# Second feed-forward product: operands split at the producer and stored as pairs, Winograd sums gathered in PSUM, the output gate applied to the sums

## The chip, the core and the metric

One core of one Trainium2 chip. TensorE (PE) multiplies into PSUM, VectorE (DVE) and ScalarE (ACT) read PSUM and SBUF, GpSimd (POOL) reads SBUF only, and DMAs are issued from the queues of SyncE (SP), ScalarE and GpSimd. The metric is the device time of one execution in microseconds (us), the median of several runs.

## The reference, cut to what matters

The kernel is one layer of a token mixer (three mixers, gated sum, projection) and then this part, which the change is about:

```
def swiglu(xn, w_in, w_out):
    gate, up = jnp.split(xn @ w_in, 2, axis=-1)
    return (jax.nn.silu(gate) * up) @ w_out
...
h_lat = h_lat + gt2l * swiglu(modulate(rms_norm(h_lat, norm2), sh2l, sc2l), w_ffn_in, w_ffn_out)
return rms_norm(h_lat, norm_f)
```

There are 1024 tokens, 1024 channels and 2816 hidden columns, all float32.

## The kernel before

Each float32 operand of a matmul is split into two parts, high (a rounded copy, ACT) and low (value minus high, DVE), by `split2` (L1475). A product is then three matmuls for each 128 rows: high by high, high by low, low by high.

Both feed-forward products use Strassen's scheme in Winograd's form: a 2 by 2 block product from seven block products and additions.

**First product**, `ffn_in` (L1553). The 2816 hidden columns go by in 11 pairs of column tiles. `quad(m, w)` makes the gate half (w = 0) or the other half (w = 1) of a pair: seven products of 12 matmuls, each in a PSUM bank of its own, 168 matmuls a pair. DVE adds the products (L1626 to L1649), ACT applies silu, POOL multiplies the halves (L1608). `hidden` (L1588) forms the seven left operands of the second product from the four hidden blocks and stores them to DRAM (`hid_d`) as float32, on SP's queue.

**Second product**, `ffn_out` (L1666). The 11 pairs are the inner dimension, taken in GROUPS of 2, 3, 3 and 3 pairs. In a group there are four steps t, each a tile of 128 tokens from each half of the tokens. A step has seven products p1 to p7 of 3 matmuls a pair: 42 matmuls in a step of the first group, 63 in the others, 924 in all. `weights(i)` (L1680) loads a pair's rows, multiplies them by the gate row `bc1` on POOL (L1685), forms sums on POOL and splits seven operands. `hidden(i, t)` (L1709) loads a pair's seven left operands for a step in three pieces (`hraw`), and splits each piece into `hh` again, in every step. DVE adds up the products (L1778 to L1791), and POOL or DVE adds the result into `acc` (L1752), which starts as the residual from DRAM. The last group adds squares, the norm and the store of the output.

In step 0 of a group the products run pair by pair into seven banks, so that the first pair can start before the others' weights are there. In the other steps they run product by product.

The instruction order of each engine is set by a scheduler which works on estimated durations; each engine then runs its list strictly in order.

Of the kernel before, what the change touches and what calls it, by code (L numbers as in the profile page):

```python
# [16 lines left out]
P = 128  # L17
# [8 lines left out]
def vb(ap, n):  # L26
    """[128, a] -> [128, a, n] with a step-0 last dim."""
    return ap.unsqueeze(len(ap.shape)).to_broadcast(list(ap.shape) + [n])


def mb(ap, n):
    """[128, a...] -> [128, n, a...] with a step-0 middle dim."""
    sh = list(ap.shape)
    return ap.unsqueeze(1).to_broadcast([sh[0], n] + sh[1:])


class SplitMixin:
    def split(s, raw, hi, lo):
        """exact split of an fp32 tile into two fp32r parts, the columns (g, c) in the order (c, g)"""
        h, l = (t.rearrange("p k (c g) -> p k g c", c=16) for t in (hi, lo))  # L40
        raw = raw.rearrange("p k (g c) -> p k g c", c=16)
        s.nc.scalar.activation(h, raw, AF.Copy)
        s.nc.vector.tensor_tensor(l, raw, h, op=ALU.subtract)
        return hi, lo
# [143 lines left out]
def _parts(v, bits):  # L188
    """v as a sum of fp32 constants, all but the last with few significant bits"""
# [12 lines left out]
class S5Mixin:  # L202
    def s5_setup(s, pool, fpool, tpool):
# [45 lines left out]
        def exp_parts(x, em, ex):  # L249
            """ex = exp(x), em = exp(x) - 1"""  # L250
# [81 lines left out]
        def cmul(pr, pi, o, n_, a, b):  # L332
            """pr, pi: [o, o + n_) = [a, a + n_) times b"""
# [50 lines left out]
    def s5_u(s, q, pool, w):  # L384
        """in-projection tile of u to DRAM as [tau][(c, g)][(half, w) of the latents, chunk of the context], in pieces"""
# [103 lines left out]
    def s5_scan(s, pool):  # L489
        """scan within five blocks of 32 chunks at once, then over the blocks' ends"""  # L490
# [17 lines left out]
    def s5_carry(s, e, pool):  # L508
        """the states of blocks 1 to 4 of groups 4 e .. 4 e + 3 from those before the blocks"""
# [15 lines left out]
    def s5_toeplitz(s, h, pool):  # L525
        """within-chunk responses of half h of the groups"""
# [5 lines left out]
    def s5_back(s, e, pool):  # L532
        """outputs of groups 4 e .. 4 e + 3"""
# [35 lines left out]
    def s5_out(s, pool):  # L569
        """skip, gelu and the gated unit in the token order (t, h, w); yields between the split of the input and the products"""  # L570
# [65 lines left out]
class RwkvMixin:  # L636
    def rwkv_const(s, pool):
        """small constants that live until the last chunk step"""
# [49 lines left out]
    def shift(s, m, ctx, pool, tag, bufs=1):  # L688
        """in-projection tile m of zb after the token shift"""
# [205 lines left out]
    def rwkv_inverse(s, aq, pool, tag, E):  # L895
        """rows of -A^T on (direction, head parity, j) x unit x t -> rows of ((I + A)^-1)^T"""
# [23 lines left out]
    def rwkv_chain(s, pool, halfway):  # L920
        """the chunks in order, both directions side by side, a chunk of each in a piece"""
# [43 lines left out]
        def flush(i):  # L965
            """second halves of the outputs whose first halves were two steps ago"""
# [94 lines left out]
    def rwkv_out(s, b, ysum, pool):  # L1061
        """group norm of tokens 128 b .. 128 b + 127, then the output gate, feature-major"""
# [31 lines left out]
WTB = 6  # L1094
TV = 1
WSEQ = "w n0 w n1 n2 n3 f s0 f s1 f s2 f f s3"
AVE = (((0, 0),), ((0, 1), (1, 0)))
HB, OTB = {2: 7, 3: 4}, 5
# [15 lines left out]
class Kern(LruMixin, S5Mixin, RwkvMixin, ParamMixin, SplitMixin):  # L1114
# [9 lines left out]
    def fill(s, n, after=None):  # L1124
        """the next n pieces of the background work, behind an instruction of the tensor engine if one is given"""
# [30 lines left out]
    def front(s, pool, wpool, side, parts):  # L1156
        """normed, modulated and transposed input as split parts, with pieces of other work at its side"""
# [95 lines left out]
    def mod2(s, pool):  # L1253
        """gates of both residuals (as rows in DRAM) and the second modulation, in pieces"""
# [33 lines left out]
    def wsplit(s, src, nk, pool, tag, rb=1, hb=1, lb=1, pool_hi=False, pool_lo=False):  # L1288
        """split parts of a weight tile"""
# [11 lines left out]
    def mm3(s, ps, whi, wlo, ahi, alo, nk):  # L1301
        """ps = sum over k of w[k]^T a[k] from the split parts"""
# [4 lines left out]
    def mm3s(s, ps, whi, wlo, ahi, alo, nk):  # L1307
        """the same in pieces of three, yields between them"""
# [9 lines left out]
    def in_wp(s, m, pool):  # L1318
        """split parts with the columns (g, c) in the order (c, g)"""
# [15 lines left out]
    def zg(s):  # L1335
        """the gates of the branches, in pieces of three matrix products"""
# [15 lines left out]
    def half(s, ap, h):  # L1352
        """tokens 256 .. 767 (h = 0) or the others of [128, 1024]"""
# [4 lines left out]
    def branch_y(s, y_d, h):  # L1358
        """split parts of half h of a branch input: [:, 0] and [:, 1]"""
# [10 lines left out]
    def branch(s, br, m, h, w, yt, wpool, out=None):  # L1370
        """gated product of a branch for half h of the tokens, in pieces of three matrix products"""
# [12 lines left out]
    def branches(s, acc, y0, wpool):  # L1384
        """the branches a and c, their gated sum to acc[m][half]"""
# [12 lines left out]
    def branch_b(s, h, acc, mg, wpool):  # L1398
        """last branch for half h of the tokens: split parts of the merged branches"""
# [12 lines left out]
    def yb_part(s, b, o):  # L1412
        """split parts of block b of the second half of the tokens"""
# [6 lines left out]
    def yb_last(s):  # L1420
        """the blocks 1 and 6, before 0 and 7 come straight from the chain"""
# [16 lines left out]
    def row_bc(s, pool, j):  # L1438
        """row of a gate (0, 1) or of the last norm (2) on every partition"""
# [7 lines left out]
    def wo_load(s, ring, quarters):  # L1447
        """split parts of the output weights, s.wo[half of the columns][row tile] = (hi, lo)"""
# [26 lines left out]
    def split2(s, raw, hl, eng=None):  # L1475
        """split parts (hi, lo) of a tile"""
# [4 lines left out]
    def wout(s, h, mg, wpool):  # L1481
        """output projection of half h of the tokens onto the residual; yields after two products"""
# [17 lines left out]
    def wnorm(s, h, t, wpool, parts, y):  # L1500
        """second norm of a token tile, modulated and transposed, to y(q)"""
# [29 lines left out]
    def wsum(s, t, wpool, parts, y):  # L1531
        """sums of the halves for a token tile"""
# [20 lines left out]
    def ffn_in(s, parts, ring, epool, tp):  # L1553
        """hidden tiles of the feed-forward, by Strassen's scheme (Winograd's form) on halves of the tokens, halves of
        the rows and pairs of column tiles; yields between the first products, then after a pair"""
# [4 lines left out]
        def product(b, name):  # L1560
            ps = s.mm()
            hi, lo = parts(name)
            seq = [(w, a, k) for k in range(4) for w, a in ((b[0], hi), (b[0], lo))] + [(b[1], hi, k) for k in range(4)]
            for n, (w, a, k) in enumerate(seq):
                nc.tensor.matmul(ps, w[:, k], a[:, k], start=n == 0, stop=n == len(seq) - 1)  # L1565
# [16 lines left out]
        def etmp():  # L1582
            return epool.tile([P, 512], F32, name="fe", tag="fe", bufs=4)

        def tmp(pool=None):
            return (pool or s.tl).tile([P, 512], F32, name="ft", tag="ft", bufs=2 if pool else 8)

        def hidden(i, g):  # L1588
            """the operands of the second product from the hidden tiles, in the places of the gates"""
            (a11, f0), (a12, f1), (a21, _), (a22, f2) = g[0, 0], g[1, 0], g[0, 1], g[1, 1]  # L1590
            G.tensor_tensor(f0, a11, a21, op=ALU.subtract)
            V.tensor_tensor(a21, a21, a22, op=ALU.add)
            V.tensor_tensor(f2, a21, a11, op=ALU.subtract)
            G.tensor_tensor(f1, a12, f2, op=ALU.subtract)
            for c, v in enumerate((a11, a12, f2, f0, a21, a22, f1)):
                nc.sync.dma_start(s.hid_d[i][:, :, c], v.rearrange("p (t c) -> p t c", t=4))

        def quad(m, w, g, tp=None):
            """columns of the tiles m and m + 1 of the gates (w = 0) or of the others (w = 1)"""
# [3 lines left out]
            def done(j, h, v):  # L1603
# [3 lines left out]
                else:  # L1607
                    G.tensor_tensor(v, v, g[j, h], op=ALU.mult)  # L1608
                    g[j, h] = v, g[j, h]

            def sums(pool):
# [4 lines left out]
                e.tensor_tensor(t[3], t[1], b21, op=ALU.subtract)  # L1616
# [5 lines left out]
            S.activation(p1, product(operand(b11), "a11"), AF.Copy)  # L1622
            if early:
                yield
            c11 = etmp() if early else tmp()
            V.tensor_tensor(c11, p1, product(operand(b21), "a12"), op=ALU.add)  # L1626
            done(0, 0, c11)
# [412 lines left out]
```

## Time and profile before

| | us |
|---|---|
| median of 3 runs | 2371.12 |
| lowest, highest | 2370.62, 2376.17 |
| profiled execution, its span | 2372.2 |
| TensorE busy in the span | 2103.7 (89%) |
| DVE busy in the span | 1729.6 (73%) |
| first feed-forward product on TensorE | 1623.3 to 2061.6 |
| second, to the end of its matmuls | 2061.4 to 2362.5 |

Busy shares over the whole span hide that the two products have different limits, so the stretches are read apart. A matmul of 512 columns is pipelined with the next: its duration in a list of instructions is longer than its share of a dense stretch.

### The profile page before, as it was taken

Reading aid. Unit: us, or ns where it says so; the run is one execution under the profiler, and the core shown is the slowest. Engines: PE = TensorE matmul, PEld = TensorE weight load, DVE = VectorE, ACT = ScalarE, POOL = GpSimd, SP = SyncE. Lnnn points to the kernel's source line nnn. Section 1 sums busy time; section 2 is a strip of 40 time slices with the busy share of each in tenths; the row PEclk is TensorE's granted clock in tenths of the full one; section 3 lists DMA queues with packets and bytes.
Section 4 is the critical chain, followed back from the end, with each engine's and each line's share of the span. In section 5 each row is a group of like instructions: output and inputs, shape, how many; then the busy total and the mean of one; then the engine's idle time right before and its main releaser. Section 6 shows DMA issues by size and latency. Waiting matters only on the chain.

```text
span 2372.2 us, 38912 instructions
## 1 busy us (share of the span) xinstructions
PE 2103.7 (89%) x14441; PEld 1663.8 (70%) x14441; DVE 1729.6 (73%) x2435; ACT 930.5 (39%) x1791; POOL 1176.5 (50%) x1283
## 2 busy tenths in 40 slices
PE   5989978887999988987799999897999999978888
PEld 3868766665888777866576676685888888755666
DVE  5556688988657878899833368738856666699998
ACT  5313344532435545554434234344332333233333
POOL 3651489955323576774000133535645454467664
PEclk8989998998999989997799999998999999989889
DMA  6634322223743444546868676632433232353333
GB/s 250 167 108 120 84 69 86 78 80 75 172 134 108 137 133 123 152 126 180 222 164 191 158 206 163 217 109 91 129 89 111 89 111 89 119 177 107 114 115 123
DMA packets 404379, 313.05 MB, mean 132 GB/s; under 512 B 67608, under 2 KB 369887, under 8 KB 403167
## 3 DMA queue, kind: packets, MB, share of 16 engines
q1 hardware_dynamic: 400606, 299.04, 44.7%
q10 hardware_dynamic: 2880, 10.49, 1.2%
q8 instruction: 114, 1.87, 0.4%
q0 software_dynamic: 704, 1.05, 0.2%
q14 instruction: 75, 0.61, 0.1%
HBM read 216.15 MB, written 94.35 MB: 131 GB/s over the span
## 4 chain that ended last, share of the span: by engine, by line
PE 46%; DVE 24%; POOL 10%; DMA 9%; issue 7%; ACT 3%; SPq 1%; DVEq 0%; POOLq 0%; ACTq 0%
PE mm L1565 17%; PE mm L1305 7%; PE mm L1311 7%; DVE hh L1479 3%; PE cg L1011 2%; DVE wt L1479 2%; PE mm L1735 2%; PE cu L998 2%; PE cg L985 2%; DMA wm<-in_w_mod_dram 2%; DMA hraw<-hidd 1%; PE cy L1026 1%; POOL s L214 1%; POOL nt L911 1%; DVE macc L1271 1%
## 5 line engine op out<-in xcount | busy, mean ns | idle before, releaser
L1565 PE MATMUL mm<-q,wt 128*128 128x512 f32 x1584 | 376.7, 398 | 4.5 <-DVE q L1479 3.5
L1565 PEld LDWEIGHTS mm<-q,wt 128*128 128x128 f32 x1584 | 299.6, 189 | 77.5 <-DVE q L1479 4.0
L1735 PE MATMUL mm<-wt,hh 128*128 128x512 f32 x924 | 248.9, 427 | 52.3 <-DVE wt L1479 12.1
L1735 PEld LDWEIGHTS mm<-wt,hh 128*128 128x128 f32 x924 | 184.5, 204 | 116.5 <-DVE wt L1479 18.1
L1305 PE MATMUL mm<-xh,wh 128*128 128x512 f32 (+1 forms) x576 | 215.0, 381 | 9.4 <-ACT ya L180 7.2
L1305 PE MATMUL mm<-xl,wh 128*128 128x512 f32 (+1 forms) x576 | 214.7, 380 | 1.2 <-DVE xl L1221 1.2
L1311 PE MATMUL mm<-xh,zh 128*128 128x512 f32 x384 | 160.4, 418 | 7.9 <-ACT zge L1347 5.1
L1311 PE MATMUL mm<-xl,zh 128*128 128x512 f32 x384 | 159.0, 414 | 0.0
L1305 PE MATMUL mm<-xh,wl 128*128 128x512 f32 (+1 forms) x576 | 139.9, 380 | 9.3 <-DVE wl L1298 7.0
L1478 ACT ACTIVATE wt<-wT 128x512 fp32r<-128x512 f32 x132 | 81.5, 628 | 160.6 <-PE mm L1565 129.0
L1479 DVE TENSOR_TENSOR wt<-wT,wt 128x512 fp32r<-128x512 f32 x132 | 135.7, 1035 | 2.6 <-ACT wt L1478 1.7
L1305 PEld LDWEIGHTS mm<-xh,wh 128*128 128x128 f32 x576 | 114.2, 198 | 29.8 <-ACT ya L180 8.0
L1305 PEld LDWEIGHTS mm<-xl,wh 128*128 128x128 f32 x576 | 113.8, 198 | 19.5 <-DVE xl L1221 1.5
L1311 PE MATMUL mm<-byt,bwh 128*128 128x512 f32 x384 | 118.7, 428 | 7.9 <-ACT bwh L1297 2.5
L1479 DVE TENSOR_TENSOR hh<-hraw,hh 128x256 fp32r<-128x256 f32 (+1 forms) x132 | 119.1, 925 | 8.6 <-ACT hh L1478 8.6
L1311 PE MATMUL mm<-xh,zl 128*128 128x512 f32 x384 | 110.7, 425 | 16.2 <-DVE zl L1298 16.2
L1305 PEld LDWEIGHTS mm<-xh,wl 128*128 128x128 f32 x576 | 102.1, 195 | 30.0 <-DVE wl L1298 8.7
L1015 DVE TENSOR_TENSOR x<-cg,pcend 64x256 f32<-64x256 f32 x152 | 63.9, 421 | 78.6 <-PE cg L1011 36.1
L1295 POOL CAST bwh<-bwr 128x512 fp32r<-128x512 f32 x16 | 10.0, 624 | 209.2 <-PE mm L1311 111.6
L1478 ACT ACTIVATE hh<-hraw 128x256 fp32r<-128x256 f32 (+1 forms) x132 | 56.2, 447 | 145.4 <-DMA hraw<-hidd 121.0
L1271 DVE SCALAR_TENSOR_TENSOR macc<-wm,cs,macc 128x256 f32<-128x256 f32 x112 | 87.6, 782 | 24.5 <-DMA wm<-in_w_mod_dram 22.2
L1311 PEld LDWEIGHTS mm<-xh,zl 128*128 128x128 f32 x384 | 76.2, 203 | 36.2 <-DVE zl L1298 18.7
(437 smaller groups left out, 5081.8 us busy)
## 6 DMA issues: line engine op xcount, KB each, us to landing
wt<-in_w_ffn_in_dram SPq DMA_DIRECT2D x44, 512.0 KB
hidd<-ft SPq DMA_DIRECT2D x75, 256.0 KB
wm<-in_w_mod_dram SPq DMA_DIRECT2D x64, 256.0 KB
gyl<-gyl SPq DMA_DIRECT2D x32, 512.0 KB
wr<-in_w_in_dram SPq DMA_DIRECT2D x27, 512.0 KB
zr<-in_w_in_dram SPq DMA_DIRECT2D x24, 512.0 KB
sgd<-zge SPq DMA_DIRECT2D x48, 256.0 KB
bsg<-sgd SPq DMA_DIRECT2D x48, 256.0 KB
```

Source lines behind the costliest of these rows:

```text
L214: G.tensor_tensor(o, a, b, op=op)
L985: s.pe = nc.tensor.matmul(ps[32 * q : 32 * q + 32, 64 * p : 64 * p + 64], gy[:, 2 * p + par, c - cb, 0:32], st["x"][:, p, par, :], start=T ...
L998: s.pe = nc.tensor.matmul(ps[o : o + 32, 64 * p : 64 * p + 64], st["tt"][32 * q : 32 * q + 32, p, st["cc"], :], st["gs"][32 * q : 32 * q + ...
L1011: s.pe = nc.tensor.matmul(sn[64 * par : 64 * par + 64, 64 * p : 64 * p + 64], sd[:, st["cc"], 2 * p + par, :], st["x"][:, p, par, :], star ...
L1015: V.tensor_tensor(xn[0:64, :, par, :], sn[r].rearrange("p (a k) -> p a k", a=4), vb(s.pcend[r, d, :, st["c"]], 64), op=ALU.mult)
L1271: nc.vector.scalar_tensor_tensor(acc, wm[:, j], s.cs[:, k + j, 0:1], acc, op0=ALU.mult, op1=ALU.add)
L1305: s.nc.tensor.matmul(ps, w(k), a(k), start=n == 0, stop=n == len(seq) - 1)
L1311: s.nc.tensor.matmul(ps, w[:, k], a[:, k], start=n == 0, stop=n == len(seq) - 1)
L1478: s.nc.scalar.activation(hi, raw, AF.Copy)
L1479: (eng or s.nc.vector).tensor_tensor(lo, raw, hi, op=ALU.subtract)
L1565: nc.tensor.matmul(ps, w[:, k], a[:, k], start=n == 0, stop=n == len(seq) - 1)
L1735: nc.tensor.matmul(ps, hid[k][c][h], w[k][name][b], start=start and n == 0, stop=stop and n == len(seq) - 1)
```

## The change

The seven left operands are split once, in `ffn_in`, where they are made (`fh`, two tiles), and stored as high and low parts side by side. `ffn_out` loads the seven pairs of parts of a pair and step by one DMA of 896 KB on POOL's queue into `hh` (four tiles), with no split. DVE makes one more of the operands' sums. Products that are added are accumulated by TensorE into one PSUM bank (A, B and C), from which DVE and ACT read between the products; a sign is moved into a weight sum for that. In `ffn_out` the gate row multiplies the finished sums in the last group and not the weights, `acc` starts as the first group's sums, and the residual is added in the last group. Step 0 keeps a bank for each product. The buffer counts change: WTB, the silu and sum tiles, OTB.

```diff
-WTB = 6
-TV = 1
+WTB = 5
+FHB = 2
-AVE = (((0, 0),), ((0, 1), (1, 0)))
-HB, OTB = {2: 7, 3: 4}, 5
+AVE = (((0, 1),), ((0, 1), (1, 0)))
+HB, OTB = 4, 6
...
+        def hidden(i, v, f):
+            a11, a12, a21, a22 = v[0, 0], v[1, 0], v[0, 1], v[1, 1]
+            V.tensor_tensor(f[0], a11, a21, op=ALU.subtract)
             V.tensor_tensor(a21, a21, a22, op=ALU.add)
+            V.tensor_tensor(f[1], a21, a11, op=ALU.subtract)
+            G.tensor_tensor(f[2], a12, f[1], op=ALU.subtract)
+            for c, v in enumerate((a11, f[1], a12, f[0], a21, a22, f[2])):
+                hl = s.tf.tile([P, 4, 2, P], F32R, name="fh", tag="fh", bufs=FHB)
+                s.split2(v.rearrange("p (t c) -> p t c", t=4), (hl[:, :, 0], hl[:, :, 1]))
+                nc.sync.dma_start(s.hid_d[i][:, :, c], hl.bitcast(F32))
...
-            V.tensor_tensor(c11, p1, product(operand(b21), "a12"), op=ALU.add)
-            done(0, 0, c11)
-            V.tensor_tensor(p1, p1, product(operand(t[1], op), "s2"), op=ALU.add)
-            V.tensor_tensor(u3, p1, product(operand(t[2], op), "s3"), op=ALU.add)
...
+            B = product(operand(t[1], op), "s2", stop=False)
+            u2, u3 = tmp(), tmp()
+            V.tensor_tensor(u2, p1, B, op=ALU.add)
             if not early:
+                done11(product(operand(b21), "a12", A))
+            product(operand(t[2], op), "s3", B, stop=early)
+            V.tensor_tensor(u3, p1, B, op=ALU.add)
+            C = product(operand(t[0], op), "s1", stop=False)
...
+            V.tensor_tensor(u3, u3, C, op=ALU.add)
+            done(1, 1, u3)
             if not early:
+                product(operand(t[3], op), "a22", B)
+                c21 = tmp()
+                V.tensor_tensor(c21, p1, B, op=ALU.add)
+                done(0, 1, c21)
+            product(operand(b22), "s4", C)
+            V.tensor_tensor(u2, u2, C, op=ALU.add)
+            done(1, 0, u2)
...
-                G.tensor_tensor(r, r, bc1.rearrange("p (n c) -> p n c", n=2), op=ALU.mult)
...
         def hidden(i, t):
-            for c0, n in ((0, 2), (2, 2), (4, 3)):
-                raw = pa.tile([P, n, P], F32, name="hraw", tag="hraw", bufs=4)
-                nc.sync.dma_start(raw, s.hid_d[i][:, t, c0 : c0 + n])
-                hl = (pa if n == 2 else pb).tile([P, 2, n, P], F32R, name="hh", tag=f"hh{n}", bufs=HB[n])
-                s.split2(raw, (hl[:, 0], hl[:, 1]))
+            hl = pb.tile([P, 7, 2, P], F32R, name="hh", tag="hh", bufs=HB)
+            G.dma_start(hl, s.hid_d[i][:, t])
...
+                    V.tensor_tensor(o, o, bc1[:, sl], op=ALU.mult)
+                    (V if t == 3 else G).tensor_tensor(o, o, res[h][:, sl], op=ALU.add)
...
+                    add(0, 0, None, product("p2", A))
+                    product("p7", B, stop=False)
+                    V.tensor_tensor(u3, p1, B, op=ALU.add)
+                    C = product("p5", stop=False)
+                    add(1, 1, u3, C)
+                    product("p4", B)
+                    add(1, 0, p1, B)
+                    product("p3", C)
+                    add(0, 1, u2, C)
```

**TensorE in the second group of pairs, where one step ends and the next begins.** `hh` is a tile of left operands, `wt` an operand of the weights, `mm` a bank; "waits" names whom the instruction waits for, DMASW a DMA of POOL's queue. TensorE's list before the change:

```order
L1735 MATMUL mm_19818<-wt_19495,hh_19710 128x512 [waits DVE_49]
L1735 MATMUL mm_19818<-wt_19495,hh_19710 128x512 x2
L1735 MATMUL mm_19818<-wt_19529,hh_19725 128x512 x3
L1735 MATMUL mm_19818<-wt_19563,hh_19740 128x512 x3
L1735 MATMUL mm_19876<-wt_19470,hh_19832 128x512 [waits DVE_49]
L1735 MATMUL mm_19876<-wt_19470,hh_19832 128x512 x2
L1735 MATMUL mm_19876<-wt_19504,hh_19847 128x512 x3
```

The old step ends with nine matmuls on three tiles, and the new one starts on `hh` tiles of its own.

TensorE's list at the same place with the change, the nine matmuls of p3 and the first ones of the next step:

```order
L1750 MATMUL mm_19637<-wt_19427,hh_19586 128x512 [waits DVE_49]
L1750 MATMUL mm_19637<-wt_19427,hh_19586 128x512 x2
L1750 MATMUL mm_19637<-wt_19459,hh_19588 128x512 x3
L1750 MATMUL mm_19637<-wt_19491,hh_19590 128x512 x3
L1750 MATMUL mm_19680<-wt_19434,hh_19673 128x512 [waits DMASW3_49]
L1750 MATMUL mm_19680<-wt_19434,hh_19673 128x512 x2
L1750 MATMUL mm_19691<-wt_19442,hh_19673 128x512 x3
L1750 MATMUL mm_19722<-wt_19452,hh_19673 128x512 x3
L1750 MATMUL mm_19680<-wt_19466,hh_19675 128x512 [waits DMASW4_49]
```

The first wait of a step was for DVE's split and is now for a DMA; the tile it fills is one that the last nine matmuls of the step before still read.

**POOL at the same place.** `wT` is a sum of weights, `ot` a sum of products. POOL's list before the change:

```order
L1752 TENSOR_TENSOR acc2_19002<-acc2_19002,ot_19343 128x512 [waits DMAHW2_49,DVE_49]
L1699 TENSOR_TENSOR wT_19511<-wor2_19501,wT_19510 128x512 [waits Pool_49]
L1701 TENSOR_TENSOR wT_19512<-wor2_19501,wor2_19498 128x512
L1752 TENSOR_TENSOR acc2_19002<-acc2_19002,ot_19327 128x512 [waits DVE_49]
L1752 TENSOR_TENSOR acc2_19002<-acc2_19002,ot_19346 128x512 [waits DMAHW0_49,DVE_49]
```

POOL only adds here; the loads of left operands stood in SP's list.

POOL's list at the same place with the change:

```order
L1779 TENSOR_TENSOR acc2_19090<-acc2_19090,ot_19594 128x512 [waits DVE_49]
L1726 DMA hh_19673<-hidd_82 128x1792 [waits DMASW7_49,PE_49]
L1779 TENSOR_TENSOR acc2_19090<-acc2_19090,ot_19592 128x512 [waits DVE_49]
L1726 DMA hh_19675<-hidd_82 128x1792 [waits DMASW0_49,PE_49]
L1726 DMA hh_19756<-hidd_82 128x1792 [waits DMASW1_49,PE_49]
L1719 TENSOR_TENSOR wT_19881<-wor2_19875,wT_19881 128x512 [waits DVE_49]
```

Between POOL's additions now stand DMAs that wait for TensorE to leave a tile.

**ACT in the first product, a late pair.** `fe` is the copy of the first product, `ft` a hidden or gate tile. ACT's list before the change:

```order
L1622 ACTIVATE fe_18103<-mm_18107 128x512 [waits PE_49]
L1478 ACTIVATE wt_18397<-wt_18392 128x512 [waits DMAHW0_49]
L1478 ACTIVATE wt_18415<-wt_18394 128x512 [waits DMAHW2_49,PE_49]
L1605 ACTIVATE ft_18121<-ft_18121 128x512 [waits DMAHW1_49,DVE_49]
L1478 ACTIVATE wt_18325<-wT0_18281 128x512 [waits PE_49]
```

ACT only copies a product, applies silu and splits weights here.

ACT's list at about the same place with the change:

```order
L1478 ACTIVATE fh_18141<-ft_17979 128x4x128 [waits DMAHW6_49,DVE_49]
L1478 ACTIVATE fh_18145<-ft_18045 128x4x128 [waits DMAHW7_49,Activation_49,Pool_49]
L1618 ACTIVATE ft_18229<-mm_18173 128x512
L1478 ACTIVATE wt_18381<-wT0_18322 128x512 [waits PE_49,Activation_49]
L1478 ACTIVATE wt_18399<-wT3_18325 128x512 [waits PE_49]
L1478 ACTIVATE fh_18149<-ft_17910 128x4x128 [waits DMAHW2_49,DVE_49]
```

Among the weights' splits now stand splits of the pair before, each of which waits for the store (DMAHW) that empties one of the two `fh` tiles.

## Rows read from the trace of the kernel before

**Rows 1.** Stretches: each engine's busy us (instructions), granted clock, DMA share, GB/s

```profile
1660.00:2061.00 401.00, 401.00 (x1727) 323.79 (x1726) 259.33 (x315) 124.37 (x209) 206.22 (x142) 1.00 0.35 104
2061.00:2372.00 311.00, 249.27 (x927) 184.65 (x925) 296.40 (x355) 111.91 (x249) 193.59 (x132) 0.89 0.41 128
```

**Rows 2.** TensorE in order of time: start, length, matmuls [idle before <-releaser]

```profile
2061.40 1.80 PE L1735 MATMUL mm<-wt,hh 128*128 128x512 f32 x7
...
2069.53 7.60 PE L1735 MATMUL mm<-wt,hh 128*128 128x512 f32 x20 [4.89 <-DVE wt L1479]
...
2083.23 7.58 PE L1735 MATMUL mm<-wt,hh 128*128 128x512 f32 x22 [0.91 <-ACT wt L1478]
...
2115.50 5.96 PE L1735 MATMUL mm<-wt,hh 128*128 128x512 f32 x18 [2.46 <-DVE ot L1789]
...
2258.38 9.50 PE L1735 MATMUL mm<-wt,hh 128*128 128x512 f32 x33 [2.47 <-DVE hh L1479]
...
2314.62 47.92 PE L1735 MATMUL mm<-wt,hh 128*128 128x512 f32 x202 [1.70 <-DVE wt L1479]
```

**Rows 3.** Groups by line and shape, 2061 to 2372: busy us, mean ns

```profile
L1479 DVE TENSOR_TENSOR hh<-hraw,hh 128x256 fp32r<-128x256 f32 x82 | 73.5, 908 | 5.5 <-ACT hh L1478 5.5
...
L1752 POOL TENSOR_TENSOR acc<-acc,ot 128x512 f32<-128x512 f32 x44 | 63.2, 1444 | 53.4 <-DVE ot L1785 32.0 <-DVE ot L1789 7.1 <-DVE ot L1778 5.6
L1479 DVE TENSOR_TENSOR wt<-wT,wt 128x512 fp32r<-128x512 f32 x44 | 55.7, 1280 | 0.3
L1685 POOL TENSOR_TENSOR wor<-wor,wt 128x1024 f32<-128x1024 f32 x20 | 52.6, 2630 | 23.1 <-DMA wor<-in_w_ffn_out_dram 21.5 <-DVE hh L1479 1.6
L1479 DVE TENSOR_TENSOR hh<-hraw,hh 128x384 fp32r<-128x384 f32 x44 | 42.6, 989 | 3.1 <-ACT hh L1478 3.1
...
L1699 POOL TENSOR_TENSOR wT<-wor,wT 128x512 f32<-128x512 f32 x10 | 14.7, 1473 | 0.4
...
L1788 DVE TENSOR_TENSOR ot<-ot,mm 128x512 f32<-128x512 f32 x16 | 10.8, 676 | 0.0
```

**Rows 4.** Groups by line and shape in the first product, 1700 to 2040

```profile
L1479 DVE TENSOR_TENSOR wt<-wT,wt 128x512 fp32r<-128x512 f32 x70 | 61.6, 880 | 0.6
...
L1592 DVE TENSOR_TENSOR ft<-ft 128x512 f32<-128x512 f32 x9 | 15.9, 1766 | 4.3 <-POOL ft L1591 4.3
...
L1637 DVE TENSOR_TENSOR ft<-fe,mm 128x512 f32<-128x512 f32 x18 | 12.4, 689 | 25.0 <-PE mm L1565 25.0
```

**Rows 5.** Chain that ended last, in order of time: start, us, what

```profile
2073.02 3.59 DMA wor<-in_w_ffn_out_dram
```

**Rows 6.** DMAs of POOL's queue, tile lru_bd (32 KB each): issue ns, landing

```profile
L125 POOL DMA_DIRECT2D lru_bd<-in_lru_wa_dram x8: 607/621/748, 273.7 to 466.4; - x8
...
DMA to landing us min/median/max: 2.0/2.1/4.2
```

**Rows 7.** The same for tile craw (128 KB each)

```profile
L370 POOL DMA_DIRECT2D craw<-in_s_c_re_dram x2: 762/889/1016, 76.3 to 77.3; - x2
...
DMA to landing us min/median/max: 6.0/6.1/6.4
```

**Rows 8.** Stretches of 5 us: loads of long rows, then stores

```profile
10.00:15.00 5.00, 4.37 (x24) 1.56 (x24) 1.44 (x2) 2.21 (x6) 0.75 (x2) 1.00 1.00 409
...
1870.00:1875.00 5.00, 5.00 (x23) 4.05 (x22) 3.79 (x4) 1.79 (x4) 2.97 (x2) 1.00 0.76 214
```

**Rows 9.** End of the span in order of time, DVE and ACT

```profile
2363.71 0.68 DVE L1791 TENSOR_TENSOR ot<-ot,mm 128x512 f32<-128x512 f32 x1
...
2365.20 0.63 ACT L1757 ACTIVATE ot<-acc 128x512 f32<-128x512 f32 x1 [0.60 <-DVE acc L1752]
...
2367.77 1.42 DVE L1768 SCALAR_TENSOR_TENSOR acc<-acc,rs,wt 128x512 f32<-128x512 f32 x2 [0.44 <-POOL rs L1764]
```

## Prediction before the run

> **What bounds the kernel now.** I first read the busy time of each engine by stretch [rows 1]. In the first product, 1660 to 2061, TensorE is busy 401 of 401 us with 1727 matmuls at granted clock 1.00, so one matmul costs 401/1727 = 0.232 us, and DVE has room (259 of 401). In the second, 2061 to 2372, DVE is busy 296 of 311 us, TensorE only 249, and the mean granted clock is 0.89. The first product is bound by TensorE, the second by DVE.
>
> Next, TensorE in order of time [rows 2]. The second product's 924 matmuls at 0.232 would take 214.5 us; from 2061.6 to the span's end at 2372.2 it is 310.6. TensorE idles 1 to 5 us at a time, mostly released by DVE, and after a pause it is slow for a while: 18 matmuls in 5.96 us instead of 4.2 (+1.8), 33 in 9.50 instead of 7.6 (+1.9), 20 in 7.60 instead of 4.6 (+3.0), on average 2.2 us a pause. I read that as part of them at the lower clock level (1.2 of 2.4 GHz); the mean of 0.89 agrees. Where DVE has no splits left, 202 matmuls run in 47.92 us, 0.237 each: this is what the rest could reach.
>
> Last, the groups of that stretch [rows 3]. DVE spends 73.5 + 42.6 = 116.1 us on 126 low parts of `hh`, the operands that each step loads and splits again.
>
> **What the change removes (second product).** DVE loses the 116 us of splits, ACT their high parts, POOL the gate's 20 multiplications (52.6 us) and 21 of 44 additions into `acc` at 1.44 us [rows 3]. DVE's sums stay about as many (one or two more in all). DVE is then busy about 296 − 116 = 180 us plus last-group additions, of some 290: no longer the bound. What is late next are TensorE's waits for `hh`.
>
> **First product.** A pair of tiles takes TensorE 168 × 0.232 = 39.0 us. Its DVE instructions go from 30 to 35: seven splits more (0.95 us, between the 0.88 of a weight's split [rows 4] and the 0.99 of an `hh` split [rows 3]) and `f0` (up to the 1.77 of such a sum beside POOL), less four PSUM sums of 0.69 [rows 4]; 25.2 us (259/401 × 39) become 25.2 + 6.6 + 1.8 − 2.8 = 30.8. To this come waits in order: a split waits until the store from its `fh` tile, two splits back, has landed. A store is 512 KB; the dense stretch with stores moves 214/0.76 = 282 GB/s of full engine share [rows 8], so 1.9 us, plus 2.1 us fixed from the smallest landing [rows 6]: 4.0. With ACT's half ahead, the next use of a tile can start 4.9 us after a split. By DVE's list the fourth split of a pair has 2.5 us of other work since the split two before, so it waits 2.4; the sixth waits 1.5; the others are covered. 30.8 + 3.9 = 34.7 of 39.0 stays behind TensorE. But sums that share a bank must be read within one product (12 × 0.232 = 2.8 us), and a split that waits stands ahead of some of them, on DVE and, for its high part, on ACT: I add 0.4 us for each of ten pairs, **+4 us** (0 to 37, see the third rival).
>
> **Start of the second product.** T is the end of the first, 2061.6. Before, 42 matmuls of the first step were done at 2083.23 + 10/22 × 7.58 = 2086.7 [rows 2], T + 25. Afterwards the first `hh` DMA stands in POOL's list behind the last hidden operand and weight sums. The weight load (3.59 us [rows 5], issued about T − 1) gives T + 3; three POOL instructions at 1.47 [rows 3] T + 7.5; the DMA (4.3, below) T + 12; 21 matmuls at 0.33 (those at 2083 and 2069 took 0.34 and 0.38 [rows 2]) T + 19. The second pair's operands come behind the last six `fh` splits, at about T + 17, and then seven weight splits of 1.2 (1.28 [rows 3], some ready): T + 25. So 42 are done at **T + 26** (23 to 29): nothing gained there.
>
> **The new wait.** Four `hh` tiles serve steps of three pairs, and a step reads each of its tiles until p3, its last product. So the next step's second and third operands can be loaded only when p3 has read a tile. TensorE has six matmuls (1.4 us) left then inside a group, nine (2.1) at a change of groups. This happens at eight places: six steps inside the three-pair groups, two changes of group; elsewhere the fourth tile, or step 0's order by pairs, lets the load go early. The trace has no 896 KB load on POOL's queue. Lower bound of its landing: the fastest small one on that queue, 2.1 us for 32 KB [rows 6], plus 885 KB at 409 GB/s, what a stretch of long rows moved at DMA share 1.00 [rows 8], 2.2: **4.3**. Upper: as `craw` on the same queue, 6.1 us for 128 KB [rows 7], plus 768 KB/409 = 1.9: 8.0. I take 4.3, since `hh`'s rows are long like those of the 409 GB/s. With 0.2 from TensorE's release to the issue, the wait inside a group is 4.5 − 1.4 = 3.1, plus 0.3 since POOL adds into `acc` between two issues, and 4.5 − 2.1 = 2.4 at a change. With 2.2 of slow matmuls behind each pause [rows 2]: 6 × 5.6 + 2 × 4.6 = **42 us**. Bounds: 25 if the clock holds, and 42 + 8 × 3.7 = 72 by the upper landing. Queued behind the issues on POOL are `acc` additions and the next group's weight sums; they cost nothing while POOL, freed of 52.6 + 30 us, has time, and I set **5 us** (0 to 15) for what waits in order anyway.
>
> **End.** From the last sum of a product to the end of the span it is now 2372.2 − 2362.5 = 9.7 us. Four DVE instructions like that of 0.68 [rows 9] join it (gate, residual, for two halves): **12.5**.
>
> **The sum.** From T: 26 + 882 × 0.232 (204.6) + 42 + 5 + 12.5 = 290.1, against 310.6: −20.5. With +4 of the first product −16.5. The profiled span is 2372.2, 1.1 above the median 2371.12, to which the difference is applied: 2371.1 − 16.5 = 2354.6, **2355 us**. About 0.3% (7 us) is what a measurement can tell from no change, so 2364 to 2378 counts as the same.
>
> **Rivals.**
> *Better: the clock holds* through pauses of 2 to 3 us and in-order waits vanish. For it: 202 matmuls ran at 0.237 after a pause of 1.70; against: each 2.5 us pause above was followed by slow ones [rows 2]. 42 falls to 25, 5 to 0, 4 to 0: 2355 − 26 = 2329. Chance 0.17.
>
> *Slower: POOL's loads land like `craw`.* At 8.0 instead of 4.3, eight waits and the first load cost 3.5 us more each, 31: 2386. It turns from faster to slower at a landing of 4.3 + 16.5/8 = 6.4 us. For it: `craw` and `lru_bd` are the nearest DMAs of that queue, and 128 KB took 6.0 at least [rows 7]; against: those are issued from the kernel's start, with other transfers beside them. Chance 0.16. On how POOL's queue could be slow, issues on it took 0.61 to 0.75 us for `lru_bd` [rows 6] and up to 1.02 for `craw` [rows 7], so no issue here was held up for long. The Trainium skill, SBUF — State Buffer, section "A bandwidth-pool intuition that's wrong", says that a DMA issued by GpSimd of about 620 ns alone takes about 3100 ns beside a DVE `tensor_copy`, because its descriptors cannot be written meanwhile; its "Who interferes with whom" exempts DVE's `tensor_tensor` from that mode, though not from contention where both inputs lie in SBUF. DVE runs almost only such two-input instructions here, so by that price the estimate would be +20 us at eight places, 2375; this sum does without it.
>
> *Slower: the stores bind the first product.* They double, on an SP queue that also loads weights. If a store takes 8.0 us, twice 4.0, the two waits of a pair become 6.4 and 5.5 by the same list: 30.8 + 11.9 = 42.7 of 39.0, +37 over ten pairs in place of +4: 2388. The point is at about 7 us a store. For it: DMA share is already 0.76 in a stretch with stores [rows 8]; against: 0.35 on the mean [rows 1]. Chance 0.13.
>
> *No effect:* DVE is freed, but POOL's and DVE's in-order lists hold the weights' sums behind DMAs that wait for TensorE, and the pauses stay as long as now: about 2371. Chance 0.07.
>
> **How the numbers follow.** The forecast has 0.47 (its own range 2340 to 2372, by start ±3, waits of 25 to 50, in-order waits of 0 to 15). Faster by over 0.3%: 0.37 of it, 0.16 of the better rival, 0.02 of the two slower ones, together 0.55. Same: 0.09 of the forecast, 0.01 of the better rival, 0.06 of "no effect", 0.06 of the two slower ones, 0.22. Slower: 0.21 of the two slower ones, 0.01 each of the forecast and of "no effect", 0.23. The range takes in the better rival with its start 3 to 7 us better, and both slower ones as priced: 2322 to 2390.
>
> **What would show it.** In the stretch of the second product DVE's busy share falls below 0.7 and no split of `hh` is left; TensorE's pauses are eight of 3 to 4 us released by a DMA into `hh`, and the next matmuls are slow; 42 matmuls are done at T + 26. In the first product TensorE stays at 0.232 us a matmul and clock 1.00; if not, the third rival holds, and pauses there are released by `ft` sums behind `fh` splits. An `hh` landing over 6.4 us makes the second. If many pauses are released by DVE or POOL weights still, the sum's 5 us is wrong.

## The result, and the profile after

The changed kernel takes 2400.73 us (median of 4 runs, 2397.26 to 2402.31) against 2370.87 of the kernel before: ratio 1.0117, 95% interval 1.0099 to 1.0136. It is slower by 1.2%; the forecast was 2355 us, faster. The profiled execution has a span of 2400.1 us, 27.9 longer than before.

The two stretches after the change, columns as in [rows 1] (busy us and instructions of PE, its weight loads, DVE, ACT, POOL, then granted clock, DMA share, GB/s):

```profile
1660.00:2061.00 401.00, 400.39 (x1724) 323.16 (x1723) 286.06 (x360) 160.51 (x277) 179.83 (x123) 1.00 0.45 146
2063.00:2400.00 337.00, 248.06 (x926) 189.28 (x924) 186.36 (x234) 68.12 (x129) 145.11 (x146) 0.87 0.54 187
```

The first product is as before: clock 1.00, 1724 matmuls in 401 us. In the second, DVE went from 296 us to 186 as forecast, and is idle almost half of the time; but the stretch is 26 us longer and TensorE no busier. DVE was freed, and TensorE got nothing of it. What it waits for now (releaser, us in total, times, longest), in the second product:

```profile
PE mm L1750 <- DMA hh<-hidd: 57.9, 12, 18.5
PE mm L1750 <- DVE ot L1816: 11.4, 6, 6.5
PE mm L1750 <- ACT wt L1478: 4.1, 1, 4.1
```

TensorE in order of time, as in [rows 2]:

```profile
2081.88 6.64 PE L1750 MATMUL mm<-wt,hh 128*128 128x512 f32 x21 [18.50 <-DMA hh<-hidd]
2092.64 12.38 PE L1750 MATMUL mm<-wt,hh 128*128 128x512 f32 x39 [4.11 <-ACT wt L1478]
2105.42 12.88 PE L1750 MATMUL mm<-wt,hh 128*128 128x512 f32 x54 [0.40 <-DMA hh<-hidd]
2124.77 24.90 PE L1750 MATMUL mm<-wt,hh 128*128 128x512 f32 x96 [6.48 <-DVE ot L1816]
2153.82 14.96 PE L1750 MATMUL mm<-wt,hh 128*128 128x512 f32 x57 [4.15 <-DMA hh<-hidd]
...
2182.50 13.09 PE L1750 MATMUL mm<-wt,hh 128*128 128x512 f32 x45 [3.87 <-DMA hh<-hidd]
...
2227.19 10.26 PE L1750 MATMUL mm<-wt,hh 128*128 128x512 f32 x32 [3.23 <-DMA hh<-hidd]
...
2311.78 10.23 PE L1750 MATMUL mm<-wt,hh 128*128 128x512 f32 x32 [6.67 <-DMA hh<-hidd]
...
2383.08 4.48 PE L1750 MATMUL mm<-wt,hh 128*128 128x512 f32 x18 [0.78 <-DVE ot L1816]
```

Nine pauses of 3 to 7 us are released by a load into `hh`, and behind each the matmuls are slow: 45 in 13.09 us instead of 10.4. One such step change, POOL and TensorE in order of time:

```profile
2173.78 4.85 PE L1750 MATMUL mm<-wt,hh 128*128 128x512 f32 x20
...
2177.53 0.58 POOL L1726 DMA_DIRECT2D hh<-hidd  x1 [1.42 <-PE mm L1750]
2178.13 1.28 POOL L1779 TENSOR_TENSOR acc<-acc,ot 128x512 f32<-128x512 f32 x1
...
2179.35 1.11 POOL L1726 DMA_DIRECT2D hh<-hidd  x2
...
2182.50 2.08 PE L1750 MATMUL mm<-wt,hh 128*128 128x512 f32 x4 [3.87 <-DMA hh<-hidd]
```

POOL itself waits for TensorE to leave the tile, issues the load at 2177.53, and TensorE, which has 1.1 us of p3 left, stands until 2182.50. It is the same where a group begins; POOL at 2222 and at 2303:

```profile
2222.16 0.58 POOL L1726 DMA_DIRECT2D hh<-hidd  x1 [4.52 <-PE mm L1750]
...
2303.31 0.58 POOL L1726 DMA_DIRECT2D hh<-hidd  x1 [4.53 <-PE mm L1750]
```

There too POOL is idle until TensorE lets go, and TensorE starts again 5.0 us and 8.5 us after the issue. The loads of `hh` (issue ns, then us to landing):

```profile
L1726 POOL DMA_DIRECT2D hh<-hidd x44: 527/577/652, 2075.9 to 2367.9; - x44
...
DMA to landing us min/median/max: 4.7/6.3/13.4
```

Against the terms of the forecast, from T, the end of the first product, which is 2063.4 now:

| us | forecast | measured |
|---|---|---|
| first product, from its first matmul (438.3 before) | +4 | 440.8, +2.5 |
| T to 42 matmuls done | 26 | 2092.64 + 21/39 × 12.38 − T = 35.9 |
| 882 matmuls at 0.232 | 204.6 | 204.6 |
| waits for `hh` behind those 42 | 25 | 39.4 |
| slow matmuls (busy time over 0.232 each) | 17 | 30.0 |
| other waits | 5 | 14.3 |
| last matmul to the end | 12.5 | 12.6 |
| second product | 290 | 336.7 (before: 310.6) |

### The profile page after: what moved, and what is told of

The parts are those of the page before. It is cut to its first block, busy times and chain, and to the rows that moved or that the text cites. A ratio compares the mean times of both kernels' runs of the same rounds, so it can differ in the third digit from the quotient of the medians.

```text
span 2400.1 us, 38306 instructions
## 1 busy us (share of the span) xinstructions
PE 2107.7 (88%) x14441; PEld 1674.3 (70%) x14441; DVE 1645.3 (69%) x2355; ACT 922.9 (38%) x1739; POOL 1103.8 (46%) x1278
## 4 chain that ended last, share of the span: by engine, by line
PE 47%; DVE 19%; POOL 13%; DMA 10%; issue 7%; ACT 3%; SPq 1%; DVEq 0%; POOLq 0%; ACTq 0%
PE mm L1567 17%; PE mm L1305 7%; PE mm L1311 6%; PE mm L1750 4%; PE cg L1011 2%; PE cu L998 2%; DMA wor<-in_w_ffn_out_dram 2%; PE cg L985 2%; DMA hh<-hidd 1%; POOL nt L911 1%; POOL nt L909 1%; DVE wt L1479 1%; PE cy L1026 1%; POOL s L214 1%; DMA wm<-in_w_mod_dram 1%
## 5 line engine op out<-in xcount | busy, mean ns | idle before, releaser
L1479 DVE TENSOR_TENSOR wt<-wT,wt 128x512 fp32r<-128x512 f32 x132 | 125.0, 955 | 50.9 <-ACT wt L1478 50.0
L1479 DVE TENSOR_TENSOR fh<-ft,fh 128x512 fp32r<-128x512 f32 x76 | 64.2, 856 | 61.2 <-ACT fh L1478 61.1
L1002 ACT ACTIVATE x<-cu 32x256 f32<-32x256 f32 x156 | 58.5, 375 | 101.4 <-PE cu L998 98.4
```

Of the source, the lines that this page charges most:

```text
L1002: S.activation(st["x"][96:128, :, par, :], ps[o : o + 32, 0:256].rearrange("p (a k) -> p a k", a=4), AF.Copy)
L1479: (eng or s.nc.vector).tensor_tensor(lo, raw, hi, op=ALU.subtract)
```

## The experiments

All are variants of the changed kernel unless said otherwise; ratios are to the kernel before, run on the same chip.

**e4: the split at the producer undone alone.** `ffn_in` stores one float32 tile again, SP loads it in three pieces and ACT and DVE split it in every step; shared banks and the gate on the sums stay.

```diff
-                s.split2(v.rearrange("p (t c) -> p t c", t=4), (hl[:, :, 0], hl[:, :, 1]))
-                nc.sync.dma_start(s.hid_d[i][:, :, c], hl.bitcast(F32))
+                nc.sync.dma_start(s.hid_d[i][:, :, c], v.rearrange("p (t c) -> p t c", t=4))
...
+            for c0, n in ((0, 2), (2, 2), (4, 3)):
+                raw = pa.tile([P, n, P], F32, name="hraw", tag="hraw", bufs=4)
+                nc.sync.dma_start(raw, s.hid_d[i][:, t, c0 : c0 + n])
...
+                s.split2(raw, (hl[:, 0], hl[:, 1]))
```

> The split at the producer alone is undone: operands stored once as they are, loaded by SP in three pieces and split in every step; shared banks and the gate on the sums stay. Theory A (the split and its one-tile loads are the whole loss): the second product is bound by DVE again, its 116 us of splits are back, the stretch to the end takes 300 to 312 us instead of 337, the first product is back at 0.232 us a matmul, 2360 to 2373 us. Theory B (the shared banks, whose reads TensorE must wait for, are part of it): waits for DVE's sums of 10 us or more in the second product, over 2380 us.

Measured: 2365.67 us, ratio 0.9969 (0.9956 to 0.9982). So the rest of the change, the banks and the gate above all, makes the kernel 0.3% faster, and the split with its loads carries the whole loss: theory A. Of theory B's sign, 10 us or more of waits for DVE's sums, there are 14.7 us, but the kernel before, without shared banks, has 23.3. The 300 us of the second product in e4 (DVE's is the third pair of numbers):

```profile
2070.00:2370.00 300.00, 237.09 (x924) 178.28 (x922) 246.68 (x357) 112.96 (x252) 131.27 (x105) 0.92 0.44 135
```

Its `hh` splits on DVE, as groups of lines and shapes (busy us, mean ns):

```profile
L1479 DVE TENSOR_TENSOR hh<-hraw,hh 128x256 fp32r<-128x256 f32 x88 | 56.7, 652 | 33.5 <-ACT hh L1478 33.4
...
L1479 DVE TENSOR_TENSOR hh<-hraw,hh 128x384 fp32r<-128x384 f32 x44 | 35.9, 832 | 9.1 <-ACT hh L1478 9.1
```

From the end of its first product (2070.5) to the span's end (2369.9) e4 takes 299.4 us, 11 less than before; its first product takes 441.0 us, as long as the changed kernel's. The splits are back, but each is shorter: 652 ns where it was 908 [rows 3]; e7 looks at that.

**e1: left operands in three tiles.** The same bytes of SBUF and the same data, but p1, p6, p2 come in one tile, p7, p5 in the next, p4, p3 in the last, with four buffers each.

```diff
-            hl = pb.tile([P, 7, 2, P], F32R, name="hh", tag="hh", bufs=HB)
-            G.dma_start(hl, s.hid_d[i][:, t])
+            for c0, n in ((0, 3), (3, 2), (5, 2)):
+                hl = pb.tile([P, n, 2, P], F32R, name="hh", tag=f"hh{c0}", bufs=HB)
+                G.dma_start(hl, s.hid_d[i][:, t, c0 : c0 + n])
...
```

> The seven pairs of parts of a pair and step come in three tiles of three, two and two products with four buffers each, so the same memory, 132 loads instead of 44. Theory A (a tile that is held until p3 is the main loss): the waits for hh behind the first one, 39 us in 11 waits, and most of the 30 us of slow matmuls behind them go, 35 to 55 us less than the changed kernel, 2346 to 2366 us. Theory B (the in-order lists of POOL and DVE, or the transfers, are the loss): 88 more issues of 0.58 us on POOL, the waits come back under other names, less than 12 us gained, over 2388 us.

Measured: 2351.53 us, ratio 0.9902 (0.9885 to 0.9919): theory A. It is 1% faster than the kernel before. TensorE's waits in the second product of e1:

```profile
PE mm L1753 <- DMA hh<-hidd: 18.4, 3, 17.1
PE mm L1753 <- ACT wt L1478: 9.2, 2, 6.1
PE mm L1753 <- DVE ot L1819: 6.3, 5, 2.6
```

And the stretch itself:

```profile
2061.00:2345.00 284.00, 228.73 (x926) 177.39 (x924) 183.05 (x234) 66.52 (x129) 195.25 (x234) 0.92 0.73 222
```

Behind the first load (17.1 us) 1.3 us of waits for `hh` are left, of 39.4, and the busy time over 0.232 us a matmul falls from 33.3 to 14.3 us. POOL is busy for 50 us more, nearly all of it issues, and the kernel is faster all the same. The start is no better than in the changed kernel, and from the last matmul to the end it takes 19.4 us instead of 12.6.

**e5: one tile, three loads.** Tells the tile's release from the size of a load.

```diff
-            G.dma_start(hl, s.hid_d[i][:, t])
+            for c0, n in ((0, 3), (3, 2), (5, 2)):
+                G.dma_start(hl[:, c0 : c0 + n], s.hid_d[i][:, t, c0 : c0 + n])
```

> As the changed kernel with one tile of left operands for a pair and step, but its 896 KB come by three loads (384, 256, 256 KB) on POOL's queue. Theory A (what the pieces of e1 won is that a piece is free before p3): the tile is still held until p3, only the first piece lands earlier, by 1 to 2 us at each of 11 waits; waits for hh behind the first 20 to 32 us instead of 39, time 2375 to 2392 us. Theory B (the size of a load alone is what e1 changed): near e1, 2346 to 2360 us.

Measured: 2382.20 us, ratio 1.0048 (1.0030 to 1.0065). The time is theory A's; the waits are a little over its 20 to 32: 51.6 − 17.2 = 34.4 us. That is 5 us less than in the changed kernel; waits for DVE's sums fall too, from 13.0 to 5.9 us, which neither theory had. TensorE's waits for `hh` in e5:

```profile
PE mm L1751 <- DMA hh<-hidd: 51.6, 16, 17.2
```

Smaller loads into a tile that is held until p3 give back some 17 of the 50 us of e1; the rest needs pieces that are free on their own.

**e3: work for TensorE in the pause.** `zero` is an operand of zeros, so nothing is added to the sums.

```diff
+WARM = 14
...
+                        if n == 3 and name == "p1" and t in (2, 3) and not new:
+                            with s.tc.issue_after(s.p3.ins):
+                                for _ in range(WARM):
+                                    nc.tensor.matmul(ps, zero, w[0][name][0], start=False, stop=False, skip_group_check=True)
...
```

> Before the second operand tile's first matmul in steps 2 and 3 of the three-pair groups, TensorE runs 14 products with a zero operand (3.25 us of work that adds nothing) while it would wait for the load, six times. Theory A (the pause itself lowers the clock for what follows): the six stretches behind these waits lose their slow matmuls, 14 us by the trace of the changed kernel, so 9 to 14 us less, about 2389 us. Theory B (those matmuls are slow for another reason, such as the transfers at that time): stretches unchanged, 0 to 4 us more, 2400 to 2405 us.

Measured: 2395.31 us, ratio 1.0098 (1.0079 to 1.0117). TensorE at one of the six places (that of 2182.50 above):

```profile
2178.23 3.42 PE L1756 MATMUL mm<-wt,zero 128*128 128x512 f32 x14
2182.16 2.37 PE L1757 MATMUL mm<-wt,hh 128*128 128x512 f32 x9 [0.51 <-DMA hh<-hidd]
2185.12 12.91 PE L1757 MATMUL mm<-wt,hh 128*128 128x512 f32 x54 [0.59 <-DMA hh<-hidd]
```

The 63 matmuls of that step take 15.3 us instead of 17.6. Over the six steps (393 matmuls, 91.2 us at 0.232) the excess is 4.2 us instead of 15.0. The stretch behind that place in the changed kernel, then in e3 (engines first, then granted clock, DMA share, GB/s):

```profile
2182.50:2195.60 13.10, 13.09 (x45) 10.11 (x45) 3.40 (x5) 2.50 (x4) 1.72 (x1) 0.81 0.44 156
```

```profile
2182.20:2198.00 15.80, 15.21 (x64) 11.98 (x65) 5.31 (x7) 1.86 (x3) 3.50 (x4) 1.00 0.38 132
```

Over the six stretches the granted clock is 0.81 to 0.91 in the changed kernel, so part of each runs at the lower level of 1.2 GHz, and 1.00 in e3, beside about the same transfers. So the slow matmuls come from the pause, by the clock, and not from the transfers: theory A. In the total this shows only in part: the profiled span is 9.5 us shorter, but the median only 5, under the 9 expected, and the two intervals overlap. Why the median gains less is not settled.

**e2: the loads for step 1 held back at the start.** `s.flag` is written from the last pair's seventh split.

```diff
+            if i == NF // 2 - 1:
+                V.tensor_copy(s.flag, hl[:, 0, 1, 0:1])
...
+            if i < 2 and t == 1:
+                S.activation(hl[:, 0, 0, 0:1], s.flag, AF.Copy)
             G.dma_start(hl, s.hid_d[i][:, t])
```

> The two loads of hh for step 1 of the first group are held until the last pair's seventh split is made (three tiny instructions more). Theory A (these loads slow down the last stores from fh, of which one took 12.1 us, and the second pair's weight splits stand behind them): no store over 6 us, the second pair's matmuls start about 21 us behind the end of the first product instead of 29, 6 to 10 us less, about 2393 us. Theory B (something else paces the second pair's splits): that start stays within 3 us, time 2398 to 2403 us.

Measured: 2394.39 us, ratio 1.0093 (1.0071 to 1.0114), an interval that overlaps the changed kernel's; the profiled span is 2399.7. In the changed kernel the chain of work shows two of the last stores, the second of which held up the splits behind it (start, us):

```profile
2073.17 3.22 DMA hidd<-fh
...
2077.85 12.13 DMA hidd<-fh
```

The stretch of that store, engines first, then clock, DMA share and GB/s:

```profile
2076.00:2090.00 14.00, 6.64 (x21) 5.01 (x21) 1.38 (x2) 1.26 (x2) 2.18 (x4) 0.67 1.02 355
```

The chain of e2 at the same place:

```profile
2070.43 3.23 DMA hidd<-fh
...
2075.12 7.89 DMA hidd<-fh
```

TensorE of e2 in order of time:

```profile
2086.66 2.37 PE L1754 MATMUL mm<-wt,hh 128*128 128x512 f32 x9 [0.48 <-DVE wt L1479]
...
2094.94 2.36 PE L1754 MATMUL mm<-wt,hh 128*128 128x512 f32 x9 [2.52 <-DMA hh<-hidd]
...
2123.56 24.41 PE L1754 MATMUL mm<-wt,hh 128*128 128x512 f32 x96 [6.82 <-DVE ot L1820]
```

The store is 4.2 us shorter and the second pair starts 26 us behind the end of the first product (2060.7) instead of 29; both are less than theory A asked. Then step 1 waits for the loads held back, and 114 matmuls are done 56.1 us behind that end instead of 54.9. The loads and stores do compete, but moving them about gains nothing here: from the end of the first product to the end of the span e2 takes 339.0 us, the changed kernel 336.7. So by the profiled runs its lower median does not come from the start; its first product is 9.5 us shorter (431.3 us), and why is not shown.

**e6: `hh` loaded from SP's queue, one tile.**

```diff
-            G.dma_start(hl, s.hid_d[i][:, t])
+            nc.sync.dma_start(hl.bitcast(F32), s.hid_d[i][:, t])
```

> As the changed kernel, but hh is loaded from SP's queue. Theory A (POOL's queue lands late because of how it issues): a load on SP's queue takes clearly less than the 4.7 to 5.9 us that loads held TensorE for on POOL's, each of the waits behind a step is 1 us or more shorter. Theory B (the landing is the transfer's): 4.5 to 6 us as on POOL's queue and waits of 3.5 to 4.5 us; and since SP's list has the last stores and weight loads that wait for POOL ahead of them, the start is later or some loads are: 2400 to 2425 us.

Measured: 2387.07 us, ratio 1.0058 (1.0041 to 1.0075), 14 us less than the changed kernel, where 0 to 24 more were expected. Loads that held TensorE inside a group, from the chain of work of e6 (start, us):

```profile
2174.13 4.54 DMA hh<-hidd
...
2194.94 4.57 DMA hh<-hidd
...
2250.58 5.41 DMA hh<-hidd
...
2331.16 6.35 DMA hh<-hidd
...
2354.79 4.56 DMA hh<-hidd
```

The same of the changed kernel:

```profile
2177.53 4.93 DMA hh<-hidd
...
2199.74 4.80 DMA hh<-hidd
...
2257.91 5.38 DMA hh<-hidd
...
2345.06 4.86 DMA hh<-hidd
...
2367.22 4.94 DMA hh<-hidd
```

The landing is 0.2 to 0.4 us shorter on SP's queue at four of the six places inside a group (at the sixth it is 4.48 against 4.71), the same at one and 1.5 us longer at one. So there POOL's queue is not what takes the time: theory B. Also as B has it, the first load comes later (27.0 us instead of 18.5). But behind it the waits for `hh` are 59.4 − 27.0 = 32.4 us, not 39.4, and those for DVE's sums 9.8, not 13. Six of the 7 us lie at the three changes of group (2.1, 2.6 and 3.4 us instead of 4.2, 3.2 and 6.7). Neither theory had priced that, and its cause is not shown: the changed kernel's POOL was free when it issued those loads, so its weight sums did not hold them.

**e9: e1 with SP's queue from the second group on.**

```diff
+                if i < 2:
+                    G.dma_start(hl, s.hid_d[i][:, t, c0 : c0 + n])
+                else:
+                    nc.sync.dma_start(hl.bitcast(F32), s.hid_d[i][:, t, c0 : c0 + n])
```

> As e1 (three pieces), but from the second group of pairs on the pieces are loaded from SP's queue, the first group's still from POOL's. It asks whether POOL's list holds back loads that are otherwise free to start. Theory A (it does: a load stands behind weight sums and acc additions): the waits of 2 to 3 us that e1 has at the changes of group become shorter and POOL loses 108 issues of 0.54 us, 4 to 10 us less than e1, 2342 to 2348 us. Theory B (those waits come from the weights, which SP's list then delays behind loads that wait for TensorE): as e1 or up to 15 us slower, 2350 to 2367 us.

Measured: 2343.33 us, ratio 0.9864 (0.9843 to 0.9885), the fastest of all, and within theory A's range. Where it gains on e1 the trace does not settle: its profiled run is the slowest of its four and as long as e1's, waits for `hh` are longer (28.1 us in 5) and those for DVE's sums shorter (1.9 us, 6.8 in e1), and the end behind the last matmul is 13.5 us instead of 19.4. So theory A's time came, and its reason is not shown.

**e7: e4 with POOL's multiplications back, by one.**

```diff
+                G.tensor_tensor(r, r, one.unsqueeze(2).to_broadcast([P, 2, 512]), op=ALU.mult)
```

> As e4, but POOL again multiplies each loaded weight tile (128x1024), by one, 22 times: the cost of the gate on the weights without its effect. Theory A (a POOL instruction of that size holds up DVE's instructions with two SBUF inputs): the low parts of hh, 652 ns for 128x256 in e4, are back near the 908 ns of before, DVE's busy time in the second product rises by 20 us or more, 8 to 15 us more than e4, 2373 to 2381 us. Theory B (POOL's gate only cost POOL time): DVE's durations as in e4, 0 to 4 us more, 2365 to 2370 us.

Measured: 2378.01 us, ratio 1.0023 (1.0009 to 1.0038): 12.3 us more than e4. Groups of lines and shapes of e7:

```profile
L1479 DVE TENSOR_TENSOR hh<-hraw,hh 128x256 fp32r<-128x256 f32 x85 | 65.9, 781 | 25.1 <-ACT hh L1478 24.9
...
L1701 POOL TENSOR_TENSOR wor<-wor,one 128x1024 f32<-128x1024 f32 x20 | 40.4, 2019 | 48.4 <-DMA wor<-in_w_ffn_out_dram 44.6 <-DVE hh L1479 2.6 <-DVE wt L1479 1.3
```

Its 300 us of the second product:

```profile
2070.00:2370.00 300.00, 243.41 (x919) 180.06 (x919) 260.25 (x346) 110.34 (x245) 167.45 (x119) 0.92 0.41 129
```

The splits lengthen from 652 to 781 ns, DVE's time by 13.6 us: theory A in kind, at two thirds of its size, beside POOL instructions that are shorter too (2019 ns against 2630 [rows 3]). DVE's sums with one input in PSUM take 677 ns in both runs, so DVE as a whole did not get slower. How much of the 12.3 us comes from DVE, and how much from weight sums that stand behind 40 us more of work in POOL's list, the run does not separate.

**e8: e1 with the gate and the residual applied to `acc` early in the last group.**

```diff
+                    for h, n in itertools.product(range(2), range(2)):
...
+                        V.tensor_tensor(o, o, bc1[:, sl], op=ALU.mult)
+                        G.tensor_tensor(o, o, res[h][:, sl], op=ALU.add)
...
+                        if last:
+                            V.tensor_tensor(c, c, bc1[:, 512 * n : 512 * n + 512], op=ALU.mult)
```

> As e1, but in the last group acc is multiplied by the gate and gets the residual before the step's products end, and the gate then multiplies the group's sums alone, so that less stands behind the last matmul. Expected: from the last matmul's end to the end of the span 12 us or less instead of 19, 5 to 8 us less than e1, about 2345 us. If DVE's list puts the norm's instructions first again, 0 to 2 us, or more by the 16 added DVE instructions.

Measured: 2365.14 us, ratio 0.9965 (0.9950 to 0.9980), 14 us slower than e1. The end is shorter (14.8 us instead of 19.4, not the 12 expected), but DVE's list puts the early multiplications ahead of a sum that frees a bank. DVE and TensorE of e8 in order of time:

```profile
2262.13 13.54 DVE L1750 TENSOR_TENSOR acc<-acc,wt 128x512 f32<-128x512 f32 x8
...
2276.32 4.21 PE L1757 MATMUL mm<-wt,hh 128*128 128x512 f32 x9 [12.86 <-DVE acc L1786]
```

## Why the prediction was wrong

The step that failed is the price of the new wait: its mechanism was named rightly, but it cost 69 us and not 42. At the start and in the waits in order a mechanism was missing as well. Together the terms that were too small make 46 us, all to one side, where the margin was 16.5.

- **The new wait (42 forecast, 39.4 + 30.0 = 69 measured).** It is what the change lost most by: e1, with the same bytes in three tiles, takes nearly all of it away and turns 1.2% slower into 1.0% faster, and e5 shows that smaller loads alone give only a third of that. Three sizes failed. The landing of the loads behind the nine pauses was 4.7 to 5.9 us and once 8.4, 5.4 in the mean, not 4.3, the lower bound that the forecast took: 10 us in all. The places were nine, not eight: the change from the first group to the second was left out (2153.82). At a change of group POOL issued the load at once and TensorE had its nine matmuls left, both as forecast, but the loads landed in 5.9, 5.0 and 8.4 us; why the last took so long is not shown. And the slow matmuls cost 2.4 us behind each of the nine, close to the 2.2 forecast, but 8.5 us more stand behind short pauses and DVE's, which the forecast had at nothing; that they come from the pause was right (e3).
- **The start (26 forecast, 35.9 measured).** The first load let TensorE start 18.5 us behind T, not 12, since POOL's list held it behind the last hidden operands until 2075.9, and it then took 5.8 us to land, not 4.3. Then four loads of 896 KB ran beside the last stores, one of which took 12.1 us instead of 4.0, and the second pair's weight splits stood behind the splits that waited for it. e2 shows the contention, and that holding back two loads does not mend the start.
- **Other waits (5 forecast, 14.3 measured).** The largest, 6.5 us at 2124.77, is a sum on DVE that frees a bank and stands in DVE's list behind splits of the next group's weights, which wait for POOL's sums, which wait for a weight load (issued at 2110.71, POOL's sum at 2114.60, DVE's at 2124.04). The forecast had said that what is queued on POOL costs nothing while POOL has time; POOL had time, and its list still made others wait.
- **What held.** DVE's fall to 186 us, the end (12.6 us), the direction of banks and gate (e4). The first product lost 2.5 us where 4 were forecast, so the third rival is out, but that the numbers are close is luck: e4 has no splits there and takes as long, so the splits that wait are not what costs it. A gain of the size forecast is there when pieces are free on their own: from T to the end e1 takes 283.3 us, the forecast's sum was 290. It is not that sum come true, since in e1 the wait nearly goes, and the start and the end are longer than forecast.
- **The rivals.** None came as put. Of the nine loads on POOL's queue behind the pauses, eight stayed under the 6.4 us from which the second rival decides, and by e6 the queue is worth 0.4 us a load at most inside a group. The range ended at 2390 because start, landing and in-order waits were each stretched in a rival of its own and never added.
- **Slips in the working.** 6 × 5.6 + 2 × 4.6 is 42.8, not 42; the second rival takes 3.5 us a load where 8.0 − 4.3 is 3.7, which makes it 2388; and DVE loses three PSUM sums a pair, not four (its count of 35 is right). None of them bears on the outcome.

On the page quoted in the prediction (the Trainium skill, SBUF — State Buffer, "A bandwidth-pool intuition that's wrong"): issues on POOL's queue took 0.53 to 0.65 us here and inside a group the loads landed at most 0.4 us later than SP's, so a delay of the size it gives for a `tensor_copy` did not occur beside the instructions that DVE runs here.

## What to carry to other kernels

A tile is free when its last reader is done, so a tile that holds operands of several products should be cut along the order in which they are used; with the same bytes that was worth 2% here, 0.7% of it by the smaller loads alone (e5). When work is taken off a bound engine, price the lifetime of the buffers it leaves behind and the slow matmuls behind each new pause, and add the unknowns that can be true together before setting a range. An engine with idle time can still make others wait by the order of its list.

## What the runs showed of the hardware

Taking a multiplication off POOL made DVE's instructions shorter: the 128x256 split took 908 ns beside POOL's 2630 ns multiplications, 652 without them (e4) and 781 with shorter ones (e7). Only the last two differ by the multiplications alone; POOL also makes fewer additions in e4 than before. The Trainium skill, SBUF — State Buffer, "Who interferes with whom", says that a DVE instruction with two SBUF inputs contends with a GpSimd instruction that reads SBUF; the 652 and 781 ns of e4 and e7 agree. I had counted that part of the change as POOL time only.
